# A transformer-trunk layer on one Trainium2 core: another model of the engines orders the instruction queues

## The chip, the cores and the metric

The kernel runs on one core of a Trainium2 chip. The core has five engines with a queue of instructions each, which run their queues strictly in order and wait for one another through semaphores: TensorE (PE in the profile, with PEld for its weight loads), VectorE (DVE), ScalarE (ACT), GpSimd (POOL) and SyncE (SP), which only issues transfers; POOL issues some too. The metric is the device time of one execution in microseconds (us). A queue's order is fixed when the program is built, so a ready instruction waits as long as the one ahead of it on its engine does.

## What is computed

One layer of a decoder trunk over 520 columns: 512 tokens of a prompt and 8 samples of one token each, with 1024 features, in float32. Cut to its core the reference is:

```
sh1, sc1, g1, sh2, sc2, g2 = split(silu(c) @ ada_w + ada_b)
h  = rms_norm(x) * (1 + sc1) + sh1
xr, gr, q, k, v, fl, ga, gb = split(h @ w_in)
hr = rg_lru(causal_dwconv(xr))                  # gates, a scan over time
ya = (hr * gelu(gr)) @ w_proj_a
yb = attention_with_forget_gates(q, k, v, log_sigmoid(fl + b_f)) @ w_proj_b   # samples: paged cache
x  = x + g1 * ((sigmoid(ga) * ya + sigmoid(gb) * yb) @ w_o)
h2 = rms_norm(x) * (1 + sc2) + sh2
gu, up = split(h2 @ w_ffn_in)
y  = rms_norm(x + g2 * ((silu(gu) * up) @ w_ffn_out))
```

## The kernel before

Features lie on the 128 partitions (8 blocks), columns on the free axis, in two halves of 260. Each float32 product is made of three matmuls of a faster type: an operand is split into a high part (a cast) and a low part (the rest), and high x high, low x high and high x low are summed in one PSUM bank (`half_product`, L274 to L281). Weights go through the same steps all along: a transfer into `wraw` (`load_chunks`, L193; two buffers), a cast on ACT into `whi` (L226), a subtraction on DVE into `wlo` (L228; three buffers each), and then the matmuls. PSUM has 8 banks of one tag (`bank`), handed out in turn. Seven buffers of the tag `pg` serve in turn the modulation weights (`araw`), the pages of the cache (`pg`) and sums of weight blocks (`ws`).

The stages in the order of the code:

- Head. x is loaded, normalised (`ss`, `r`, `xn`), and the first two modulation vectors come from eight `araw` transfers of 512 KB for each half of the features (`first_mod`, L449, matmuls L452). `first_mod_end` copies the result (`adas`, L458), transposes it (`adaft`, L461) and makes `mod` (L465) and `n1amp` (L469). `first_h` (L475 to L480) forms `hh` and `hl`, the two parts of h, on ACT, POOL and DVE. The weights of q come through `q_weights` (L486 transfer, L493 cast, L494 subtraction), and its matmuls are at L503. `cs` is a table of constants, of which a second part (128x432) is loaded at L561.
- 50 to 120 us. The other pieces of the modulation (`ada`, transfers L332, matmuls L344), the forget logits (`pfl`, L600), weights of the gates (L865, L866), the log1p chains of the decay (L566 to L574).
- 100 to 360 us. The branch with the recurrence (`xr`, taps `xc` L934, its parts `xch` L314 and `xcl` L315, gate matmuls L955, the scan L979, copies to the output `rg_out` L991) and the merge gates (`ga`), while DVE multiplies the samples' key pages by q and sums them up (L702 to L707).
- 360 to 660 us. Attention, the projections, the merge, `w_o`, the second norm.
- 660 us to the end. The feed-forward layer. Its first tiles are plain: `fi0` to `fi3` and `fig2`, `fiu2`, `fig3`, `fiu3`, of which `swish` (L1469, ACT) reads the `fig` banks and `times_up` (L1473, DVE) the `fiu` banks. The others are made by `fast_tile` (matmuls L1569), seven products of sums of blocks in place of eight. For these POOL forms, once, sums of h2 for k = 0 to 3 (`h2_blocks`: `b1`, `b2` at L1542, `u` and `w` at L1543 to L1546), which ACT and DVE split into `tuh`/`twh` (L314) and `tul`/`twl` (L315), and, for each tile, sums of weight blocks `ws` (`split_block`, L241 to L244), which ACT and DVE split into `wb` (L248, L249).

The two pieces of POOL's work in that last stage are:

```
b1, b2, u, w = (slot(n) for n in ("b1", "b2", "u", "w"))
for b, (hi, lo) in ((b1, h2[k]), (b2, h2[k + 4])):
    pool.tensor_tensor(b, hi.bitcast(F32), lo.bitcast(F32), ALU.add)      # L1542
...
pool.tensor_tensor(s1, a21, a22, ALU.add)                                 # L241, ws
```

What sets the order: the code issues instructions for all engines in program order, with a few orders written out by hand (`issue_after` on page loads and some subtractions); then the framework's scheduler decides, when the context of L1680 closes, in which order each engine's queue holds them, respecting all data and buffer dependencies. It does so with a model of how long each instruction takes.

## Time and profile before

| what | value |
|---|---|
| median of three runs | 1056.56 us (1054.35 to 1057.24) |
| span of the profiled execution | 1055.0 us |
| mean granted TensorE clock in it | 0.982 |
| TensorE busy | 1005.1 us, 95% |
| DVE, ACT, POOL busy | 74%, 50%, 29% |

The time of the profiled execution itself is not among the three; its span runs from its first instruction to its last. Views used below are the page of this execution; the table of busy time by stretches (each row gives the stretch, its length, busy us and the instruction count of each engine, the granted clock, the DMA engines' share and GB/s); and the order of work on each engine (start, duration, engine, line, operation, output and inputs, shapes, count; in square brackets the idle time ahead of it and what ended that). SPq rows are transfers being issued by SP's queue; their duration is the issuing, not the transfer.

### The profile page before, as it was taken

How to read it: one execution, taken by the hardware profiler on the slowest of the kernel's cores; microseconds unless marked ns; L12 is line 12 of the kernel's file. 1: busy time of each engine (PE TensorE's matmuls, PEld its weight loads, DVE VectorE, ACT ScalarE, POOL GpSimd, SP SyncE). 2: the span in 40 equal slices, each digit the busy share in tenths (PEclk: the TensorE clock that was granted, in tenths of full speed). 3: DMA queues.
4: the chain of work that ended last, by engine and by line, in shares of the span. 5: the costliest groups of instructions: out<-in, count | busy, mean ns of one | idle time of the engine just before them, and what ended most of it. 6: DMA issues, size and time to landing. Idle time of an engine off the chain costs nothing.

```text
span 1055.0 us, 21248 instructions
## 1 busy us (share of the span) xinstructions
PE 1005.1 (95%) x8054; PEld 929.9 (88%) x8054; DVE 777.6 (74%) x1370; ACT 530.0 (50%) x1070; POOL 310.3 (29%) x419
## 2 busy tenths in 40 slices
PE   4999999999999999999999999997999999999993
PEld 1788899999898988878888989987999999999993
DVE  4547999988989978867655547748578558869663
ACT  3523665847671467668783235525244324524351
POOL 0324511112133245644400014383134024223114
PEclk8999999999999999999999999998999999999997
DMA  9887987788888999886865852221343233233212
GB/s 320 294 298 283 299 282 221 261 244 266 275 236 310 338 311 291 297 278 209 278 227 189 311 166 71 56 65 61 100 111 91 90 111 104 68 116 102 83 51 82
DMA packets 165354, 206.98 MB, mean 196 GB/s; under 512 B 9842, under 2 KB 126082, under 8 KB 165186
## 3 DMA queue, kind: packets, MB, share of 16 engines
q1 hardware_dynamic: 148530, 152.52, 46.0%
q0 software_dynamic: 13040, 46.67, 13.3%
q10 hardware_dynamic: 3680, 6.42, 1.7%
q8 instruction: 63, 1.03, 0.4%
q14 instruction: 41, 0.34, 0.1%
HBM read 192.49 MB, written 13.09 MB: 195 GB/s over the span
## 4 chain that ended last, share of the span: by engine, by line
PE 73%; DVE 10%; ACT 5%; DMA 4%; issue 3%; POOL 3%; SPq 0%; POOLq 0%; DVEq 0%; ACTq 0%
PE fo L281 11%; PE fi_S L1569 7%; PE fi_A L1569 6%; PE pb L281 4%; PE gb L281 4%; PE pa L281 4%; PE k L281 3%; PE ga L281 3%; PE v L281 3%; PE fiu L281 3%; PE fig L281 3%; PE wo L281 3%; PE gr L281 2%; PE xr L281 2%; PE pv L791 2%
## 5 line engine op out<-in xcount | busy, mean ns | idle before, releaser
L226 ACT CAST whi<-wraw 128x1024 fp32r<-128x1024 f32 (+2 forms) x113 | 111.5, 987 | 188.1 <-PE fo L281 45.1
L228 DVE TENSOR_TENSOR wlo<-wraw,whi 128x1024 fp32r<-128x1024 f32 (+2 forms) x113 | 134.9, 1194 | 50.5 <-ACT whi L226 43.9
L281 PE MATMUL fo<-ach,whi 128*128 128x260 f32 x302 | 85.7, 284 | 0.0
L281 PE MATMUL fo<-ach,wlo 128*128 128x260 f32 x302 | 85.2, 282 | 0.0
L281 PE MATMUL fo<-acl,whi 128*128 128x260 f32 x302 | 85.1, 282 | 0.0
L658 POOL DMA_DIRECT2D pg<-in_cache_k_dram x74 | 39.4, 533 | 142.7 <-DVE S L707 70.3
L241 POOL TENSOR_TENSOR ws<-wraw 128x512 f32<-128x512 f32 x13 | 17.6, 1350 | 200.5 <-DMA wraw<-in_w_fi_dram 197.2
L706 DVE TENSOR_TENSOR pg<-pg,qb 128x1024 f32<-128x1024 f32 x48 | 58.0, 1227 | 1.9 <-DMA pg<-in_cache_k_dram 1.8
L707 DVE TENSOR_REDUCE S<-pg 128x16 f32<-128x1024 f32 x48 | 57.0, 1207 | 0.1
L281 PEld LDWEIGHTS fo<-ach,whi 128*128 128x128 f32 x302 | 56.9, 188 | 0.2
L281 PEld LDWEIGHTS fo<-ach,wlo 128*128 128x128 f32 x302 | 56.9, 188 | 0.0
L281 PEld LDWEIGHTS fo<-acl,whi 128*128 128x128 f32 x302 | 56.8, 188 | 0.0
L1191 POOL TENSOR_SCALAR p<-p,mu 128x128 f32<-128x128 f32 (+3 forms) x28 | 36.4, 1310 | 47.9 <-DVE mu L1187 31.1
L1569 PE MATMUL fi_A<-h2h,wb 128*128 128x260 f32 x208 | 40.2, 294 | 8.7 <-ACT sw L1469 8.7
L249 DVE TENSOR_TENSOR wb<-ws,wb 128x512 fp32r<-128x512 f32 x52 | 44.3, 862 | 3.9 <-ACT wb L248 3.7
L373 POOL TENSOR_TENSOR ss<-ss,sq 128x260 f32<-128x260 f32 x18 | 13.6, 755 | 111.0 <-ACT sq L372 110.6
L248 ACT CAST wb<-ws 128x512 fp32r<-128x512 f32 x52 | 31.4, 620 | 24.0 <-issue 7.3
L1185 ACT ACTIVATE p<-p,mu 128x128 f32<-128x128 f32 (+3 forms) x64 | 35.3, 552 | 15.3 <-DVE mu L1184 15.0
L1569 PEld LDWEIGHTS fi_A<-h2h,wb 128*128 128x128 f32 x208 | 33.8, 199 | 9.0 <-ACT sw L1469 9.0
L248 ACT CAST wb<-wraw 128x512 fp32r<-128x512 f32 x39 | 23.8, 619 | 33.7 <-PE fo L281 18.1
L1396 DVE SCALAR_TENSOR_TENSOR x<-fo,mod,x 128x252 f32<-128x252 f32 x32 | 15.3, 477 | 32.9 <-PE fo L281 32.9
L1569 PE MATMUL fi_S<-twh,wb 128*128 128x260 f32 x208 | 38.4, 285 | 0.0
(436 smaller groups left out, 4068.5 us busy)
## 6 DMA issues: line engine op xcount, KB each, us to landing
araw<-in_ada_w_dram SPq DMA_DIRECT2D x48, 512.0 KB, 7.2
wraw<-in_w_fi_dram SPq DMA_DIRECT2D x44, 512.0 KB, 5.1
pg<-in_cache_k_dram POOLq DMA_DIRECT2D x42, 512.0 KB, 6.0
pg<-in_cache_v_dram SPq DMA_DIRECT2D x42, 512.0 KB, 4.7
wraw<-in_w_in_dram SPq DMA_DIRECT2D x34, 512.0 KB, 8.2
wraw<-in_w_in_dram SPq DMA_DIRECT2D x11, 1024.0 KB, 9.9
pg<-in_cache_v_dram POOLq DMA_DIRECT2D x22, 512.0 KB, 6.1
pg<-in_cache_k_dram POOLq DMA_DIRECT2D x32, 256.0 KB, 5.6
```

Of the source, the lines that this page charges most:

```text
L226: state["act"] = act.copy(hi[:, :k1 - k0], src)
L228: state["last"] = dve.tensor_tensor(lo[:, :k1 - k0], src, hi[:, :k1 - k0].bitcast(F32), ALU.subtract)
L248: state["act"] = act.copy(t[:, :4], src)
L249: state["last"] = dve.tensor_tensor(t[:, 4:], src, t[:, :4].bitcast(F32), ALU.subtract)
L281: state["mm"] = pe.matmul(out[:, :HALF], lhsT=wt[k], rhs=at, start=k == 0 and m == 0, stop=k == nk - 1 and m == 2)
L658: done.append(eng.dma_start(pg, cache[bass.ds(r, 1), :, c0:c1].rearrange("a p c -> (a p) c")))
L706: dve.tensor_tensor(pg, pg, q, ALU.mult)
L707: last = dve.tensor_reduce(S[r // 2][:, c:c + H], pg.rearrange("p (h d) -> p h d", d=DH), AX.X, ALU.add)
L791: pe.matmul(pv[0][32 * gq:32 * gq + 32, :], lhsT=pw[r][:, c:c + 32], rhs=pgs[gq // 2][:, 512 * hf:512 * hf + 512], start=j == 0, stop=j == ...
L1185: act.activation(p[:, :n + 128], p[:, :n + 128], AF.Exp, bias=mu[:, 0:1], scale=-1.0, accum_out=mu[:, 1:2])
L1191: (pool.tensor_scalar(p, p, mu[:, 2:3], None, ALU.mult) if a and i + 1 < KT else act.activation(p, p, AF.Copy, scale=mu[:, 2:3]))
L1569: state["mm"] = pe.matmul(b, lhsT=wt[k], rhs=at, start=k == 0 and m == 0, stop=k == 3 and m == 2)
```

## The change

```
-    with tile.TileContext(nc) as tc:
+    with tile.TileContext(nc, schedule_with_timeline_sim=True) as tc:
         tile_trunk_kernel(tc, *args)
```

The option makes the scheduler order the queues by a more detailed model of the engines in time. The instructions, their tiles and their transfers are the same; only ACT has two loads of a function table fewer (35 instead of 37), since functions of one table stand together more often. What differs is the place of an instruction on its own engine's queue. In the new program about one in ten of PE's instructions and most of those of DVE, ACT, POOL and SP up to 730 us stand in another place, by a few places mostly; behind that the orders of DVE, ACT and POOL are the same but for details.

The places that the prediction speaks of, in the order of the new queues:

SP, at the head (in the order before, all eight `araw` of the first half came first, then the three `wraw`, then the next `araw`, and `cs` came after these):

```
araw x7   L449
wraw x3   L486
cs        L561
araw      L449   (the eighth of the first half)
b_f, pvm
araw x6   L449   (second half)
wraw x3   L486
araw x2   L449
araw x4   L332   (ada), then x2
flr, araw, gates' weights x2, wraw (L193), gates' weights x6, qd x3, araw, araw, qd, araw
```

PE, before `pfl`: `ada` on six `araw` (L344), then `pfl` (L600) twice; before, one pair of these `ada` stood behind `pfl`, one behind the next q products, and one 13 us later.

POOL, from 672 us (before: all of k = 0 up to the second `w`, then `ws` L241, `u` of k = 0, `ws` L242 to L244, then k = 1 to 3, with the second set's L241 ahead of the last `u` and L242 to L244 behind it):

```
ws L241, ws L243               (first set; need wraw)
b1, b2 of k = 0, ws L242, u, w, ws L244, w, u
ws L241, ws L243               (second set; need the next wraw)
b1, b2 of k = 1, ws L242, u, w, ws L244, w, u
b1, b2, u, w, w, u of k = 2
b1, b2, u, w, w, u of k = 3
```

ACT, in the same stretch (before: `tuh`, `twh` of k = 0, `whi`, those of k = 1 and 2, two `wb` from `wraw`, those of k = 3, then the swish of `fig2`, and the other `wb` among what follows):

```
whi, wb x2 (from wraw), tuh, twh of k = 0, wb x4
tuh, twh of k = 1, 2 and 3
sw (swish of fig2, both halves)
```

In the middle, DVE's page products and sums (L702 to L707), the subtractions for `wlo` and `xcl`, the taps of `xc` and the scans are interleaved in another order; on ACT `rg_out` (L991) stands ahead of some casts that it stood behind; on PE the matmuls of the gates with `xcl` (L955) stand some matmuls later, inside the next `ga` product.

## The prediction

> **What bounds the kernel now.** I read the page first, then a table of busy time by stage, then the order of work on single engines where TensorE (PE) stops.
>
> ```profile
> span 1055.0 us, 21248 instructions
> PE 1005.1 (95%) x8054; PEld 929.9 (88%) x8054; DVE 777.6 (74%) x1370; ACT 530.0 (50%) x1070; POOL 310.3 (29%) x419
> PEclk8999999999999999999999999998999999999997
> ```
>
> The sum below is made against this execution's span of 1055.0 us; the median of the three runs is 1.56 us longer, which I take as what lies around the span and add at the end. PE is the bound on average. Where it is not, the table by stage tells (columns: stretch, its length, busy us and instruction count of PE, weight loads, DVE, ACT, POOL; then granted clock, DMA share, GB/s).
>
> ```profile
> 0.00:60.00 60.00, 44.64 (x342) 32.23 (x343) 31.12 (x49) 26.33 (x51) 10.53 (x26) 0.91 0.86 293
> 60.00:120.00 60.00, 58.20 (x466) 50.05 (x465) 40.55 (x84) 21.88 (x46) 24.11 (x48) 1.00 0.87 299
> 120.00:180.00 60.00, 60.00 (x478) 56.11 (x477) 59.41 (x89) 36.75 (x71) 10.96 (x21) 1.00 0.82 264
> 300.00:360.00 60.00, 58.19 (x476) 54.41 (x475) 59.37 (x76) 21.01 (x34) 21.15 (x35) 1.00 0.96 294
> 660.00:720.00 60.00, 49.66 (x398) 48.60 (x397) 37.51 (x53) 22.34 (x46) 41.10 (x49) 0.95 0.20 54
> 780.00:840.00 60.00, 60.00 (x503) 60.00 (x502) 45.01 (x77) 27.57 (x52) 12.64 (x8) 1.00 0.37 106
> sum 1055.00, PE 1005.12 PEld 929.91 DVE 777.59 ACT 529.98 POOL 310.34; mean PE 55.84 PEld 51.66 DVE 43.20 ACT 29.44 POOL 17.24
> ```
>
> So PE loses 15 us at the head, 1.8 us in 60 to 120, 10.3 us in 660 to 720, and nothing from 780 on, where a 260-column matmul takes 60/503 = 0.119 us. A delay that arises before 720 cannot be made up behind it. From 120 to 360 DVE is as full as PE. Since the edit reorders queues and changes no instruction but two table loads of ACT, I went through the new order on each engine and asked at each of PE's stops, and wherever an instruction was put behind one that starts later in this trace, whether PE has to wait.
>
> **Step A, the head.** The eight `araw` transfers feed the eight steps of `adaf`; PE's wait for each ends with its landing (columns of the order of work: start, us, engine, line, operation, tiles, count, idle time before and what ended it).
>
> ```profile
> 8.11 8.57 SPq L449 DMA_DIRECT2D araw<-in_ada_w_dram  x8
> 16.72 3.65 SPq L486 DMA_DIRECT2D wraw<-in_w_in_dram  x3
> 22.43 1.08 PE L452 MATMUL adaf<-araw,silc 128*32 128x256 f32 x8 [0.27 <-DMA araw<-in_ada_w_dram]
> 23.80 1.08 PE L452 MATMUL adaf<-araw,silc 128*32 128x256 f32 x8 [0.29 <-DMA araw<-in_ada_w_dram]
> 24.95 0.37 ACT L458 COPY adas<-adaf 128x256 f32<-128x256 f32 x1 [9.20 <-PE adaf L452]
> 26.56 0.81 ACT L475 ACTIVATE hh<-xn,mod,n1amp 128x512 fp32r<-128x512 f32 x1
> 27.43 0.58 PE L503 MATMUL qp<-hh,whi 128*128 128x260 f32 x1 [1.36 <-ACT hh L475]
> ```
>
> The steps come 23.80 - 22.43 = 1.37 us apart, which is the pace of one 512-KB transfer. In the new order the eighth `araw` stands on SP behind the three `wraw` (512 KB each) and the second part of `cs` (128x432, 216 KB). At the rate of the stretch in which these land,
>
> ```profile
> 25.00:30.00 5.00, 3.26 (x12) 2.67 (x13) 3.79 (x9) 4.40 (x9) 3.16 (x6) 0.50 1.06 378
> ```
>
> 378 GB/s, the three take 3 x 1.39 us and `cs` 0.59 us, so the eighth lands 4.7 us later. The chain from 23.80 through `adas`, `adaft`, `mod`, `hh` to the first `qp` at 27.43 hangs on it whole and moves with it. Something comes back: the `whi` and `wlo` casts that now stand between the `hh` would be done already. But PE's clock is 0.50 in this stretch, and at half clock (0.238 us a matmul) the dozen `qp` matmuls that follow would hardly run faster with their weights ready, so I take back 0.3 us. Price +4.4 us; bounds 0 (if the transfers do not land in the order of issue) and 4.7. PE is full behind it, so it stays.
>
> **Step B, the pieces of `ada` (L344).**
>
> ```profile
> 74.07 1.06 PE L344 MATMUL ada<-araw,silc 128*32 128x512 f32 x8
> 87.32 1.06 PE L344 MATMUL ada<-araw,silc 128*32 128x512 f32 x8
> ```
>
> These two groups and one between them (six transfers) stand in one block ahead of `pfl` in the new order. The first three transfers move ahead of a `wraw` on SP that waits for DVE; the last three do not. Bounds 0 and 13 us (87.32 - 74.07, the last piece landing no earlier than it is used now). I take +0.5, near the lower, because A shifts PE's need by 4 us and the transfers ahead of the last are gone earlier.
>
> **Step C, 100 to 660 us.** The order moves DVE's page products, casts and tap sums past each other, ACT's copies of `rg_out` (L991) ahead of casts, and the `xcl` halves of the gate matmuls (L955) back behind some `ga` matmuls, which loosens waits such as this one:
>
> ```profile
> 282.28 0.51 PE L955 MATMUL gate<-xch,gws 128*128 128x260 f32 x2 [1.83 <-ACT gate L956]
> ```
>
> It is the same work on an engine that is 59.4 of 60 us busy, so some waits go and others come. Bounds: all of PE's losses from 60 to 660 vanish (about 8 us), or several new waits of 2 to 4 us (+15). I take +1.0, a little above nothing: at some ten places a cast is put behind an instruction that was ready later than PE needed the cast, mostly by 1 to 3 us, and A's 4 us cover most of these.
>
> **Step D, 660 to 730 us, the largest term.** PE stops because its next matmul needs a PSUM bank, and the eight are held by `fig2` to `fiu3` until ACT's swish (L1469) reads the first.
>
> ```profile
> 709.24 0.28 PE L281 MATMUL fiu<-h2l,whi 128*128 128x260 f32 x1
> 718.26 0.80 PE L1569 MATMUL fi_A<-h2h,wb 128*128 128x260 f32 x2 [8.75 <-ACT sw L1469]
> 723.63 0.64 PE L1569 MATMUL fi_S<-twh,wb 128*128 128x260 f32 x2
> 716.77 0.62 ACT L314 CAST tuh<-u 128x520 fp32r<-128x520 f32 x1 [6.11 <-POOL u L1546]
> 717.83 0.66 ACT L1469 ACTIVATE sw<-fig 128x260 f32<-128x260 f32 x2
> 672.96 2.62 POOL L1542 TENSOR_TENSOR b<-h2h,h2l 128x520 f32<-128x520 f32 x2
> 677.31 0.92 POOL L1545 TENSOR_TENSOR w<-b,u 128x260 f32<-128x260 f32 x1
> 688.94 1.28 POOL L241 TENSOR_TENSOR ws<-wraw 128x512 f32<-128x512 f32 x1 [10.71 <-DMA wraw<-in_w_fi_dram]
> 699.09 0.73 POOL L1543 TENSOR_TENSOR u<-b 128x260 f32<-128x260 f32 x1
> 711.38 1.18 POOL L1543 TENSOR_TENSOR u<-b 128x260 f32<-128x260 f32 x1
> 716.01 0.73 POOL L1546 TENSOR_TENSOR u<-b,w 128x260 f32<-128x260 f32 x1
> 716.70 1.27 POOL L242 TENSOR_TENSOR ws<-ws,wraw 128x512 f32<-128x512 f32 x1
> 719.63 1.74 POOL L244 TENSOR_TENSOR ws<-wraw,ws 128x512 f32<-128x512 f32 x1
> 662.83 34.87 SPq L193 DMA_DIRECT2D wraw<-in_w_fi_dram  x6
> 681.84 1.23 DVE L228 TENSOR_TENSOR wlo<-wraw,whi 128x1024 fp32r<-128x1024 f32 x1 [0.65 <-ACT whi L226]
> 711.89 2.35 DVE L249 TENSOR_TENSOR wb<-wraw,wb 128x512 fp32r<-128x512 f32 x2
> ```
>
> The swish is ready at 709, but stands on ACT behind the casts of `u` and `w` of block 3, which wait for POOL's last `u` (ends 716.74). POOL works without a pause from the landing of `wraw` at 688.94 to there, 27.80 us. In the new order two `ws` operations on that `wraw` (L241, L243) stand ahead of all of `h2_blocks`, so the first five operations of block 0 (672.96 to 678.23, 5.27 us) no longer fill POOL's wait of 10.71 us; and L242 to L244 of the second `ws` set (716.70 to 721.37, 4.67 us), now behind the last `u`, come ahead of it. On ACT the swish keeps its place behind those casts. The last `u` ends at 688.94 + 27.80 + 5.27 + 4.67 = 726.68: +9.9 us. The second set's `wraw` is the last of the six issues that end at 697.70, and POOL reaches it some 12 us behind 688.94, about when it lands. Behind the stall the clock restarts cold as now: the 24 matmuls from 718.26 to 723.63 take 5.4 us instead of 2.9, no new cost.
>
> Bounds by POOL's own rows: 8 `b` at 1.31, 16 short operations at 0.73 and the two sets at 5.95 give 34.1 us and +6.3; the short ones at 1.18 give 41.3 and +13.5. I take +9.9, since the same mix of DVE work runs beside it. [...]
>
> Sum: 4.4 + 0.5 + 1.0 + 9.9 = +15.8 us, a span of 1070.8 and a time of 1072.4 us (+1.5%).
>
> **The rivals.**
>
> 1. Not slower, through the landing at 688.94. If that `wraw` landed by 673, POOL's 37.74 us would end at 710.7, 6.0 us earlier than now, and pay for A to C: 1056.6; with some of the 8 us of PE's lost time from 60 to 660 gone too, down to 1049. It decides from a landing before 679 on, where D's price falls under zero. For it: POOL does stand idle there. Against it: the transfer waits for the `wlo` that ends at 683.07 and frees one of two buffers, and that part of the order is unchanged.
> 2. DVE and ACT become the bound in the middle. With DVE at 59.41 and 59.37 of 60 us, a matmul moved ahead of its cast waits in full, and a stop as long as the one in D adds 2.5 us of cold clock. Four or five of them, 10 to 15 us more: 1084. For it: `rg_out` copies wait for DVE's scan with casts behind them. Against: `xcl` is loosened, and PE's own delay from A gives the others 4 us of slack.
> 3. Only part of D is paid, because POOL's operations run at their short prices, and PE regains 4 us in the middle: 15.8 - 3.6 - 4 = +8, about 1065 and down to 1060.
> 4. The order on the queues makes no difference that counts, as each engine waits for the same data: 1056.6.
>
> **How the numbers follow.** Forecast (1065 to 1079) 0.58; rival 1 0.10; rival 2 0.20; rival 3 0.09; rival 4 0.03. A difference under 0.3% (3.2 us) cannot be told from none. Slower: 0.58 + 0.20 + 0.09 = 0.87; same: 0.03 of rival 4 and 0.02 of rival 1; faster: 0.08 of rival 1. The range 1060 to 1087 leaves out rivals 1 and 4 and the upper quarter of rival 2, 0.18 in all.
>
> **What would show it.** A: the first `qp` matmul at 32 instead of 27.4, with the eighth `adaf` step waiting for its DMA behind a wait of about 5 us. B: a wait of under 2 us ahead of `pfl`. C: PE's losses from 100 to 660 within a few us of now. D: POOL idle until the landing, its last `u` 37 to 38 us behind it, and PE's stop before the first `fi_A` at 18 to 20 us instead of 9. The stretches behind 735 should be equal but shifted. It is wrong if the stop in D does not grow, or if PE from 100 to 360 loses over 8 us more than now.

## The result, and the profile after

The changed kernel takes 1075.49 us (median of 4 runs, 1072.84 to 1077.8); the kernel before, run beside it on the same chip, 1056.08 (4 runs). The ratio is 1.0176, 95% interval 1.0153 to 1.0199: slower by 1.8%, where 1072.4 us and slower were forecast.

The page of the changed kernel, the lines that answer to those shown of before:

```profile
span 1074.2 us, 21222 instructions
...
PE 1006.2 (94%) x8054; PEld 931.7 (87%) x8054; DVE 773.6 (72%) x1370; ACT 529.3 (49%) x1068; POOL 311.7 (29%) x419
...
PEclk9899999999899999999999999996999999999997
```

Every engine has nearly the same work as before. PE has 1.1 us more of it and the span 19.2 us more, so the time is in PE's stops. Where they lie, the table of busy time by stretches of the changed kernel tells (columns as in the prediction):

```profile
0.00:60.00 60.00, 38.80 (x297) 26.66 (x297) 28.40 (x44) 24.19 (x44) 5.76 (x23) 0.89 0.89 309
60.00:120.00 60.00, 59.35 (x475) 51.50 (x474) 40.50 (x84) 21.82 (x50) 26.65 (x50) 1.00 0.87 288
...
240.00:300.00 60.00, 55.09 (x430) 50.50 (x429) 54.63 (x68) 35.64 (x64) 11.61 (x22) 0.94 0.91 289
...
480.00:540.00 60.00, 57.51 (x432) 49.18 (x432) 36.37 (x86) 42.01 (x104) 27.81 (x46) 0.97 0.73 228
...
660.00:720.00 60.00, 59.08 (x491) 58.84 (x490) 41.70 (x77) 26.37 (x55) 33.90 (x43) 1.00 0.27 71
720.00:780.00 60.00, 41.07 (x328) 40.86 (x327) 36.58 (x68) 21.18 (x41) 18.20 (x18) 0.83 0.20 62
780.00:840.00 60.00, 60.00 (x503) 60.00 (x502) 49.06 (x84) 25.67 (x50) 24.57 (x16) 1.00 0.36 98
```

The stretch 660 to 720 looks cured only because everything comes some 12 us later: its loss of 10.3 us has become one of 18.9 in 720 to 780. Stretches of fixed limits mislead once the work has moved. What can be compared is the same matmul in both traces. For each stage, the start of its first matmul on PE, from the span's start (the last row is the end of the last matmul):

| first matmul of | before, us | after, us | later by |
|---|---|---|---|
| `qp` (head) | 27.4 | 31.6 | 4.2 |
| `xr` | 96.4 | 103.3 | 6.9 |
| `ga` of tile 5 | 225.6 | 232.1 | 6.5 |
| `ga` of tile 7 | 283.5 | 293.6 | 10.1 |
| `k` of tile 6 | 488.9 | 499.6 | 10.7 |
| `k` of tile 7 | 512.1 | 525.1 | 13.0 |
| `fig2` | 686.3 | 697.8 | 11.5 |
| first `fi_A` | 718.3 | 740.0 | 21.7 |
| `fo2` | 925.4 | 946.3 | 20.8 |
| end | 1040.4 | 1059.6 | 19.2 |

By the steps of the prediction: A and B (to `xr`) 6.9 us against 4.9 forecast, C (`xr` to `fig2`) 4.6 against 1.0, D (`fig2` to `fi_A`) 10.2 against 9.9, behind it -2.5 against 0; together 19.2 against 15.8. The rows of D, POOL's first and last in its run, ACT's and PE's at its end:

```profile
700.50 1.29 POOL L241 TENSOR_TENSOR ws<-wraw 128x512 f32<-128x512 f32 x1 [15.06 <-DMA wraw<-in_w_fi_dram]
...
737.71 0.73 POOL L1546 TENSOR_TENSOR u<-b,w 128x260 f32<-128x260 f32 x1
...
738.47 0.62 ACT L314 CAST tuh<-u 128x520 fp32r<-128x520 f32 x1 [5.12 <-POOL u L1546]
739.53 0.66 ACT L1469 ACTIVATE sw<-fig 128x260 f32<-128x260 f32 x2
739.96 0.80 PE L1569 MATMUL fi_A<-h2h,wb 128*128 128x260 f32 x2 [18.93 <-ACT sw L1469]
```

POOL waits 15.06 us for the landing, works from 700.50 to 738.44 = 37.94 us (27.80 + 5.27 + 4.67 = 37.74 was the sum), ACT casts the last `u` and `w`, then comes the swish, then PE: the chain as forecast, stop included (18 to 20 us).

The rows of A:

```profile
12.63 4.27 SPq L486 DMA_DIRECT2D wraw<-in_w_in_dram  x3
16.95 2.76 SPq L561 DMA_DIRECT2D cs<-in_cst_dram  x1
19.82 0.49 SPq L449 DMA_DIRECT2D araw<-in_ada_w_dram  x1
28.02 1.08 PE L452 MATMUL adaf<-araw,silc 128*32 128x256 f32 x8 [5.82 <-DMA araw<-in_ada_w_dram]
...
31.64 0.59 PE L503 MATMUL qp<-hh,whi 128*128 128x260 f32 x1 [1.36 <-ACT hh L475]
```

The eighth `adaf` step waits 5.82 us for its transfer, and the first `qp` starts at 31.64 (32 was forecast).

### The profile page after: what moved, and what is told of

The parts are those of the page before. It is cut to its first block, busy times and chain, and to the rows that moved or that the text cites. A ratio compares the mean times of both kernels' runs of the same rounds, so it can differ in the third digit from the quotient of the medians.

```text
span 1074.2 us, 21222 instructions
## 1 busy us (share of the span) xinstructions
PE 1006.2 (94%) x8054; PEld 931.7 (87%) x8054; DVE 773.6 (72%) x1370; ACT 529.3 (49%) x1068; POOL 311.7 (29%) x419
## 3 DMA queue, kind: packets, MB, share of 16 engines
q0 software_dynamic: 13040, 46.67, 13.1%
## 4 chain that ended last, share of the span: by engine, by line
PE 75%; DVE 7%; ACT 5%; POOL 4%; DMA 4%; issue 3%; SPq 1%; POOLq 0%; DVEq 0%; ACTq 0%
PE fo L281 10%; PE fi_S L1569 7%; PE fi_A L1569 5%; PE wo L281 4%; PE pb L281 4%; PE gb L281 4%; PE ga L281 4%; PE k L281 4%; PE v L281 3%; PE xr L281 3%; PE fiu L281 3%; PE fig L281 3%; PE gr L281 2%; PE pv L791 2%; PE qp L503 2%
## 5 line engine op out<-in xcount | busy, mean ns | idle before, releaser
L228 DVE TENSOR_TENSOR wlo<-wraw,whi 128x1024 fp32r<-128x1024 f32 (+2 forms) x113 | 131.5, 1163 | 72.9 <-ACT whi L226 64.5
L241 POOL TENSOR_TENSOR ws<-wraw 128x512 f32<-128x512 f32 x13 | 17.0, 1305 | 207.8 <-DMA wraw<-in_w_fi_dram 189.6
L1569 PE MATMUL fi_A<-h2h,wb 128*128 128x260 f32 x208 | 39.8, 292 | 18.9 <-ACT sw L1469 18.9
L707 DVE TENSOR_REDUCE S<-pg 128x16 f32<-128x1024 f32 x48 | 57.1, 1205 | 0.0
L249 DVE TENSOR_TENSOR wb<-ws,wb 128x512 fp32r<-128x512 f32 x52 | 44.7, 871 | 4.3 <-ACT wb L248 4.2
L1185 ACT ACTIVATE p<-p,mu 128x128 f32<-128x128 f32 (+3 forms) x64 | 35.4, 554 | 16.3 <-DVE mu L1184 15.8
L1191 POOL TENSOR_SCALAR p<-p,mu 128x128 f32<-128x128 f32 (+3 forms) x28 | 32.9, 1187 | 35.6 <-DVE mu L1187 20.6
L281 PE MATMUL k<-hh,whi 128*128 128x260 f32 x128 | 38.1, 298 | 2.2 <-DVE ol L1238 2.2
L249 DVE TENSOR_TENSOR wb<-wraw,wb 128x512 fp32r<-128x512 f32 x39 | 34.4, 884 | 7.2 <-ACT wb L248 7.0
```

The source lines that it names most:

```text
L228: state["last"] = dve.tensor_tensor(lo[:, :k1 - k0], src, hi[:, :k1 - k0].bitcast(F32), ALU.subtract)
L249: state["last"] = dve.tensor_tensor(t[:, 4:], src, t[:, :4].bitcast(F32), ALU.subtract)
L281: state["mm"] = pe.matmul(out[:, :HALF], lhsT=wt[k], rhs=at, start=k == 0 and m == 0, stop=k == nk - 1 and m == 2)
L707: last = dve.tensor_reduce(S[r // 2][:, c:c + H], pg.rearrange("p (h d) -> p h d", d=DH), AX.X, ALU.add)
L1185: act.activation(p[:, :n + 128], p[:, :n + 128], AF.Exp, bias=mu[:, 0:1], scale=-1.0, accum_out=mu[:, 1:2])
L1191: (pool.tensor_scalar(p, p, mu[:, 2:3], None, ALU.mult) if a and i + 1 < KT else act.activation(p, p, AF.Copy, scale=mu[:, 2:3]))
```

## The experiments

Ratios are to the kernel before, run in turn with each on the same chip. `issue_after` is a hint of the order for the scheduler, which then keeps one instruction behind another on its engine; the arithmetic is never touched. Where one stage is compared, it is by the shift of its first matmul against before's trace, as in the table above:

| kernel | ratio (95% interval) | span | `qp` | `xr` | `ga` 7 | `fig2` | `fi_A` | end |
|---|---|---|---|---|---|---|---|---|
| after | 1.0176 (1.0153 to 1.0199) | 1074.2 | 4.2 | 6.9 | 10.1 | 11.5 | 21.7 | 19.2 |
| 1: after, D undone | 1.0136 (1.0105 to 1.0166) | 1070.1 | 4.5 | 8.0 | 11.1 | 13.6 | 16.6 | 15.0 |
| 2: after, head undone | 1.0149 (1.0117 to 1.0181) | 1071.2 | 0.9 | 3.2 | 6.4 | 8.2 | 18.4 | 16.2 |
| 3: after, both undone | 1.0116 (1.009 to 1.0142) | 1068.1 | 0.5 | 2.8 | 6.1 | 12.8 | 15.8 | 13.1 |
| 4: before, blocks first | 0.9936 (0.9916 to 0.9956) | 1050.3 | -1.4 | 0.0 | 1.4 | 4.2 | -4.7 | -4.7 |
| 5: after, taps first | 1.0113 (1.0087 to 1.0139) | 1065.8 | 3.9 | 4.9 | 4.0 | 3.8 | 14.1 | 10.8 |
| 6: after, `fb` first | 1.013 (1.0099 to 1.016) | 1074.3 | 3.4 | 5.3 | 8.5 | 12.5 | 21.6 | 19.0 |
| 7: before, head changed | 1.0047 (1.0024 to 1.0069) | 1063.4 | 2.5 | 3.2 | 6.5 | 9.1 | 9.3 | 8.4 |
| 8: before, swish and sets moved | 0.9951 (0.9928 to 0.9974) | 1050.9 | -0.6 | 0.7 | 1.6 | 1.5 | -7.4 | -4.1 |
| 9: before, swish moved | 1.0011 (0.9998 to 1.0024) | 1057.0 | -2.2 | -1.9 | -1.6 | 0.8 | -8.1 | 2.0 |
| 10: after, four undone | 0.9955 (0.9943 to 0.9967) | 1052.4 | 0.5 | 2.8 | 3.9 | 4.9 | -0.9 | -2.9 |

### 1. D undone

The four `ws` operations of each set go back to the place on POOL that they had before, or nearly: the first set behind `w` of k = 0, the second behind `w` of k = 3.

```
+    blocks, blocks_w, sets = {}, [], []
+        blocks_w.append(pool.tensor_tensor(w[:, L_], b2[:, R_], u[:, L_], ALU.subtract))   # L1545
-            pool.tensor_tensor(s1, a21, a22, ALU.add)
+            with tc.issue_after(blocks_w[0 if not sets else 3].ins): pool.tensor_tensor(s1, a21, a22, ALU.add)
...                                                # and so for s2, s3, s4
```

> The changed order, but POOL forms the weight sums (L241 to L244) where the kernel before has them: the first set behind the second w of block 0, the second set behind that of block 3. Nothing else moves but two or four casts beside them. Theory (the delays of the stages add on PE's path): the last u comes 27 to 29 us behind the landing of wraw instead of 37.9, PE's stop ahead of the first fi_A goes from 18.9 back to about 9 us, and the time falls by 10 us, from 1075.5 to 1065.5 (1064 to 1067). Rival (another wait stands behind this one, casts of wb or a late second transfer): the stop stays above 13 us and the time above 1069.

Measured: the last stage gives back 7.2 of its 10.2 us (`fig2` to `fi_A` +3.0, and the same in run 3), but the time falls by only 0.40%, some 4 us where 10 were expected. In its trace `fig2` starts 2.1 us later than in the changed kernel's, ahead of the place of the edit and with the same queues up to there, and 0.9 us less comes back behind `fi_A`; 7.2 - 2.1 - 0.9 = 4.2. POOL's run in the changed kernel with D undone:

```profile
702.67 1.29 POOL L241 TENSOR_TENSOR ws<-wraw 128x512 f32<-128x512 f32 x1 [11.37 <-DMA wraw<-in_w_fi_dram]
...
731.43 1.26 POOL L243 TENSOR_TENSOR ws<-wraw 128x512 f32<-128x512 f32 x1
732.65 0.73 POOL L1546 TENSOR_TENSOR u<-b,w 128x260 f32<-128x260 f32 x1
```

It takes 30.7 us instead of 27.80: 1.26 us for an L243 that in before stands behind the last `u`, and 1.6 us in longer operations. Beside them DVE (the third of the busy times) works more than in before; these stretches are POOL's run in before and in run 1:

```profile
688.90:716.80 27.90, 20.62 (x172) 20.41 (x170) 13.04 (x9) 5.58 (x10) 27.70 (x25) 0.95 0.14 38
```

```profile
702.60:733.40 30.80, 20.57 (x172) 20.36 (x170) 17.53 (x13) 7.64 (x13) 30.49 (x26) 0.90 0.20 60
```

So the mechanism is shown (the sets' place on POOL moves PE's stop), but the stage is not fully restored. That the longer operations come from the fuller DVE, whose order remains that of the change, fits these rows but was not tried by a run of its own.

### 2 and 3. The head undone, alone and with D

```
+            qw["raw"] = sp.dma_start(raw, ada_w[...])                                       # L449
+        with tc.issue_after(qw["raw"].ins): sp.dma_start(raw[:, ko:ko + 4], w_in[...])      # L486
+    with tc.issue_after(qw["raw"].ins): sp.dma_start(cs[:, C_TRI:], cst[:, C_TRI:])         # L561
```

> The changed order, but the three wraw transfers of the head and cs are issued behind the eighth araw. Theory: the first qp matmul starts at 27.5 instead of 31.6 us, PE's shift of about 5 us at 60 us is gone, and as PE is full behind it the time falls by 4.5 to 5 us, to 1070.5 to 1071. Rival (the middle is bound by DVE and pays back what the head gains): the shift is back by 300 us and the time above 1073.

> Both edits together. Theory: they add up, 15 us less than the changed kernel, 1060.5 (1059 to 1062); what is left against before, about 4 us, is the middle. Rival (each hides a part of the other): 1064 or more.

Measured: the first `qp` starts 0.9 and 0.5 us later than before instead of 4.2, and at `xr` the shift is 3.2 and 2.8 instead of 6.9. The head's order thus costs 3.7 to 4.1 us, and nothing behind it takes that back as far as `ga` 7 (6.4 and 6.1 instead of 10.1). In the time run 2 gains 0.27%, some 3 us where 4.5 to 5 were expected, and the intervals overlap; it is the stages that show it. The two edits together were expected to reach 1060.5 us and reach 1069.86: 13.1 us are still left in the profiled run, of which 10.0 come between `xr` and `fig2`, where 1.0 was forecast. Run 2 has the same queues up to there and takes 5.0, so C is more than the small term of the forecast, but its size varies from run to run. (With the head undone the scheduler also moved some places on PE, ACT, DVE and POOL, mostly up to 480 us.)

### 5 and 6. Two places in the middle

Between `ga` of tile 5 and of tile 7 the changed kernel loses 3.6 us more than before. PE, ACT and DVE around it, in the changed kernel:

```profile
289.27 0.51 PE L955 MATMUL gate<-xch,gws 128*128 128x260 f32 x2 [2.57 <-ACT xch L314]
292.12 1.24 PE L955 MATMUL gate<-xch,gws 128*128 128x260 f32 x4 [2.34 <-ACT gate L956]
288.59 0.62 ACT L314 CAST xch<-xc 128x520 fp32r<-128x520 f32 x1 [1.80 <-DVE xc L934]
...
284.34 1.22 DVE L706 TENSOR_TENSOR pg<-pg,qb 128x1024 f32<-128x1024 f32 x1
...
285.99 0.74 DVE L934 SCALAR_TENSOR_TENSOR xc<-xr,prm,xc 128x510 f32<-128x510 f32 x1
286.65 1.21 DVE L707 TENSOR_REDUCE S<-pg 128x16 f32<-128x1024 f32 x1
287.78 0.74 DVE L934 SCALAR_TENSOR_TENSOR xc<-xr,prm,xc 128x511 f32<-128x511 f32 x1
```

Read from PE back: the gate matmul waits for `xch`, that for the last tap `xc` on DVE, and the taps stand between page products and sums, which nobody needs yet. Run 5 keeps the products behind the taps of tile 7 (`state["last"]` is the instruction behind which the next page product is issued):

```
-            dve.scalar_tensor_tensor(xc[:, d:NP], xr[:, :NP - d], cw[n], xc[:, d:NP], ALU.mult, ALU.add)   # L934
+            t = dve.scalar_tensor_tensor(xc[:, d:NP], xr[:, :NP - d], cw[n], xc[:, d:NP], ALU.mult, ALU.add); state["last"] = t if i == 7 else state["last"]
```

> The changed order, but from the conv of tile 7 on DVE does the taps of xc (L934) ahead of the next page products (L706, L707) instead of behind them. Theory: the two stops of PE at 286 to 292 us (3.17 and 2.62 us between matmuls) come from xch of tile 7, which waits for the last tap; they fall to about 2.4 us in all as in the kernel before, PE's shift between gate7 and ga7 shrinks by 3 to 4 us, and the time by as much, to 1072. Rival (the table load and the sigmoids of L956 set them, whatever DVE does): the stops stay over 5 us in all and the time over 1074.

Measured: the stop at this gate is all but gone; `ga` 7 is 4.0 us late instead of 10.1. Of these 6.1 us, 2.0 were there already at `xr`, so 4.1 are this edit's. The scheduler, given it, also put the `xcl` matmuls of the gates back close to the others on PE and moved some places on the other engines, mostly up to 415 us; the matmuls that waited were those with `xch`. `fig2` too is 3.8 late instead of 11.5, and the intervals of the time are apart (1.0113 against 1.0176). The same row, with the taps first:

```profile
283.80 0.40 PE L955 MATMUL gate<-xch,gws 128*128 128x260 f32 x2
286.23 0.51 PE L955 MATMUL gate<-xch,gws 128*128 128x260 f32 x2 [0.72 <-ACT gate L956]
```

The second place lies ahead of `k` of tile 7 (2.24 us of waiting). There the chain runs back from DVE's `ol`, queued behind a `wlo`, to that one's `whi` on ACT, which stands behind the softmax of a tile (L1185), from there to DVE (L1184) and to POOL, which waits for a transfer:

```profile
508.66 1.27 SPq L658 DMA_DIRECT2D pg<-in_cache_v_dram  x2
509.98 0.42 SPq L1156 DMA_DIRECT2D fb<-ftd  x1
518.26 0.40 POOL L1158 COPY fm<-fb 128x256 f32<-128x256 f32 x1 [4.16 <-DMA fb<-ftd]
519.11 0.29 DVE L1184 CUSTOM_DVE_ANT_0 p<-f,sc 128x128 f32<-128x128 f32 x1 [3.58 <-POOL f L1160]
...
522.14 1.04 ACT L226 CAST whi<-wraw 128x1024 fp32r<-128x1024 f32 x1
525.09 0.39 PE L281 MATMUL k<-hh,whi 128*128 128x260 f32 x1 [2.24 <-DVE ol L1238]
```

The small `fb` stands on SP behind two page loads. Run 6 issues it first:

```
+            state["fb"] = (sp.dma_start(fb, ftd[hd:hd + 1, :].partition_broadcast(128)), i)   # L1156
+        fb = state.get("fb") if eng is sp else None                                           # page loads, L656
+                tc.issue_after(fb[0].ins) if fb and fb[1] == 7 else nullcontext():
```

> The changed order, but the pages that SP loads behind the last two fb (L1156) in program order are issued behind them, not ahead. Theory: the stop of 2.64 us at 522.5 ahead of k7 is the landing of fb passed on through POOL (L1160), DVE (L1184) and ACT's softmax to the cast whi behind it; it goes, and the time falls by 2 to 3 us, to 1073. Rival (the pages are then late and pv waits for them, or the cast waits for something else): no gain, 1075 or more.

Measured: from `k` of tile 6 to that of tile 7 the shift grows by 0.4 us (14.0 to 14.4) instead of 2.3, so the chain was read rightly. The median, 1072.26 us, is near the 1073 expected, but the profiled run, the longest of its four, is no shorter than the changed kernel's, since PE waited elsewhere in it:

```profile
PE pv L793 <- DMA pg<-in_cache_v_dram: 3.0, 2, 2.5
```

(3.0 us in 2 waits, the longest 2.5; the changed kernel has 0.6 in 2.) That wait lies at 359 us, 150 us ahead of the place that the edit is about, and the queues are those of the changed kernel up to 505 us: it is a page that landed later in this run (run 3 has such a wait of 2.71 us at 357 us), not the edit's price. Whether the 2 us gained at `k` show in the time, this run can't tell: the intervals of the ratio with and without the edit overlap.

### 7. The head's change made to the kernel before

```
-    first_mod(0, acc[0], range(KT))
+    first_mod(0, acc[0], range(KT - 1))
-    first_mod_end(0, acc[0])                # and first_h, moved behind the weights of q:
+    first_mod(0, acc[0], (KT - 1,))
+    first_mod_end(0, acc[0])
```

> The kernel before with one thing done: in the head the three wraw transfers of q, and their casts, stand ahead of the eighth araw, as in the changed order (cs stays behind). Theory: the eighth adaf step starts 4.2 us later (three transfers of 1.39 us), the first qp matmul at 31 to 32 us, and the time rises by 3.5 to 5 us, to 1060. Rival (PE's later waits for DVE swallow it): under 2 us, 1058 or less.

Measured: 0.47% or 5.0 us by the ratio, 3.2 us at `xr`, and 8.4 at the end of the profiled run, the longest of its five. The head's part agrees with run 2's 3.7. The rest has two sources that this run does not part: the edit also moved some queue places up to 150 us, and the middle varies from run to run (last section); the largest piece, 4.7 us between `ga` 5 and `ga` 7, is a stretch where the queues are those of before, and in it a `whi` cast on ACT waits 8.92 us for its `wraw` to land.

### 4, 8 and 9. What holds the last stage

In run 4 both sets of `ws` stand behind `w` of k = 3, in the kernel before:

```
+            with tc.issue_after(blocks_w[3].ins): pool.tensor_tensor(s1, a21, a22, ALU.add)
...                                                # and so for s2, s3, s4
```

> The kernel before with only one thing moved: on POOL both sets of weight sums stand behind the last u of the blocks of h2. Theory (PE's stop of 9 us is POOL's wait of 10.7 us passed on by the queue): the last u ends at about 699 instead of 716.7, the stop goes, the clock stays up (2.5 us more), and the time falls by 10 to 11.5 us, to 1045 (1044 to 1047). Rival (the sums of weights are then late, and the product with S2 waits for them): the stop only moves behind the first two products, and the time is 1050 or more.

Measured: `fig2` to `fi_A` falls by 8.9 us, PE's stop ahead of `fi_A` (9.02 us from matmul to matmul in before) is gone but for three waits of under 0.8 us behind it, and the kernel is faster than before by 0.64%: it beats both. The gain is 6.8 us where 10 to 11.5 were expected. POOL no longer waits for the landing with all of k = 1 to 3 queued behind it. Price of it: the short operations, now beside DVE's subtractions, take up to 1.74 us, against 0.73 to 1.20 in before.

```profile
686.74 1.74 POOL L1543 TENSOR_TENSOR u<-b 128x260 f32<-128x260 f32 x1
...
708.53 0.75 POOL L1546 TENSOR_TENSOR u<-b,w 128x260 f32<-128x260 f32 x1
...
718.58 1.62 POOL L244 TENSOR_TENSOR ws<-wraw,ws 128x512 f32<-128x512 f32 x1
```

Is the PSUM bank (the swish behind the casts) the limit, or POOL's run itself? Run 8 issues the blocks of k = 2 and 3 one tile later, so that the swish of `fig2` does not stand behind their casts, and puts the first set behind `w` of k = 1, the second behind `w` of k = 3. Run 9 makes the first of these edits alone:

```
-            if jt == PLAIN:
-                for k in range(4):
+            if jt in (PLAIN, PLAIN + 1):
+                for k in range(2 * (jt - PLAIN), 2 * (jt - PLAIN) + 2):
                     h2_blocks(k)
```

> The kernel before with the blocks of h2 for k = 0 and 1 ahead of the first set of weight sums on POOL, those for k = 2 and 3 behind it, and these two formed in program order behind the swish of fig2, so that ACT's swish does not stand behind their casts. Theory (PE's stop is a bank held by a swish that waits for POOL through ACT's queue): the first fi_A follows the last fiu at once, at 710, the clock stays up, and a wait of at most 2 us remains ahead of S2; 10 to 12 us less than before, 1045. It should beat the kernel in which only the blocks stand first (1050). Rival (POOL's total work of 38 us sets the end of the stage in any order): 1050 or more.

> The kernel before with one edit: the blocks of k = 2 and 3 are issued one tile later, so that the swish of fig2 stands on ACT ahead of their casts; POOL's order stays as before. Theory 1, the PSUM bank held by the swish alone sets the stop: the first fi_A follows the last fiu directly, and the whole stop (9.02 us from matmul to matmul) is gained, 1047 to 1048. Theory 2, POOL's run sets the stage and the swish is only where it shows: the stop moves to the first product that needs the second set's wb; L242 to L244 of that set end 4.67 us behind the last u here, against 717.6 in the run where the set stood ahead, so the stage gains less than the 5.2 us of that run, 1 to 3 us, and the time is 1053 to 1055.5.

Measured: in both the first `fi_A` follows the last `fiu` directly, and both stop some matmuls later, run 8 first and then run 9:

```profile
714.76 0.39 PE L1569 MATMUL fi_S<-twh,wb 128*128 128x260 f32 x1 [0.90 <-ACT wb L248]
...
718.21 0.58 PE L1569 MATMUL fi_S<-twh,wb 128*128 128x260 f32 x1 [3.06 <-DVE wb L249]
```

```profile
723.16 0.59 PE L1569 MATMUL fi_S<-twh,wb 128*128 128x260 f32 x1 [9.85 <-ACT wb L248]
```

In run 9 the stop at `fi_A` is gone whole (`fi_A` 8.9 us earlier from `fig2`), it comes back as 9.85 us at `fi_S`, and the time is that of before. The two rows on ACT ahead of that `fi_S`:

```profile
721.44 0.62 ACT L314 CAST tuh<-u 128x520 fp32r<-128x520 f32 x1 [10.56 <-POOL u L1546]
...
722.50 1.13 ACT L248 CAST wb<-ws 128x512 fp32r<-128x512 f32 x2
```

The `wb` that `fi_S` waits for is of the first set, which POOL had finished at 696.28; its cast stands on ACT behind those of k = 3, as the swish did, and these wait for POOL's last `u`. The product needs `tw` of k = 3 itself from its tenth matmul on. So the swish is where the stop showed, and POOL's last blocks are what released it, in before and here.

What the bank alone is worth, run 9 does not show. The scheduler moved POOL's order in it too (L241 to L243 of the second set ahead of the blocks of k = 3), so "POOL's order stays" in the expectation did not hold, and the last `u` ends at 721.41 instead of 716.74. These 4.67 us are about what PE might have gained with POOL's order kept, which is an estimate. Run 8, which frees the swish as well, was expected to beat run 4 and does not (0.9951 against 0.9936).

### 10. Four places together

The edits of runs 2, 5 and 6 and run 4's order of POOL, on the changed kernel.

> The kernel after with four edits together: the eighth araw ahead of the wraw and cs at the head, the taps of tile 7 ahead of the page products, the last fb ahead of the page loads, and both ws sets behind w of k = 3 on POOL. If the four named places carry the change's loss, each edit gives what it gave alone: head 3.7, taps 6, fb 2.5, and in 660 to 730 the 14.9 us between +10.2 and -4.7, 27 us in all: 1048 to 1052, faster than before. If the middle's loss is spread over many small waits and moves to other places when one is taken away, the head and the last stage alone give 15 to 19 us: 1056 to 1061.

Measured: 1051.0 us (1049.76 to 1054.14), 0.45% faster than before, 23 us under the changed kernel. The time is the first theory's. By stages of the profiled run it is not quite as that theory has it: against the changed kernel the stretch to `xr` gives 4.1 us, the middle 2.4 (8.5 were expected), `fig2` to `fi_A` 16.1 (14.9 expected). In the middle the two places give what they gave alone, 4.1 us at `ga` 7 and 2.3 at `k` of tile 7, but 2.1 are lost between `xr` and `ga` 5 and 1.7 behind `k` of tile 7. This profiled execution was the longest of its six, 3 us above their median.

## Why the prediction was right, and where its terms were off

**A, right.** The eighth `araw` behind four transfers moves the first `qp` by 4.2 us (4.4 forecast); undoing it alone gives back 3.4 there and 3.7 by `xr`. It repeats: the first `qp` starts at 25.2 to 27.4 us in the four traces with the old head (before, 4, 8, 9) and at 30.8 to 31.9 in the four with the new one (after, 1, 5, 6).

**B, too small, by 2.2 us in this pair.** From the first `qp` to `xr` the shift grows by 2.7 us, where 0.5 was taken. Only 0.65 us of it is the wait ahead of the sixth `ada` piece that B spoke of:

```profile
79.32 1.05 PE L344 MATMUL ada<-araw,silc 128*32 128x512 f32 x4 [0.65 <-DMA araw<-in_ada_w_dram]
```

Of the rest 1.3 us arise ahead of the first q products (`q` 5.5 us late, `qp` 4.2). The cause was not tried by a run. With the head undone the shift still grows by 2.4 us here, so most of it isn't the head's. In the same traces as under A the stretch takes 69.0 to 70.4 us in the old order and 70.0 to 72.4 in the new, so its size is not fixed by one pair.

**C, the step that failed: taken as +1.0 "a little above nothing", it measured +4.6.** The prediction counted places where a cast stands behind something late and let A's 4 us of delay cover most of them. Whether it covered the casts was not tried; the large waits that were found had other links: DVE's taps behind page products that are not urgent (run 5: 4.1 us by `ga` 7), and a small transfer behind page loads on SP, with POOL, DVE and ACT between it and the matmul that waits (run 6: about 2 us). Both are chains in which an urgent instruction stands behind one that is merely ready. These two places repeat from trace to trace, the stretch between them does not (lengths in us; before, 4, 8 and 9 have the old order of the middle):

| stretch | old order | changed order | with the place undone |
|---|---|---|---|
| `ga` 5 to `ga` 7 | 57.9 to 59.4 | 61.5 (after, 1, 2, 3, 6) | 57.4 (5, 10) |
| `ga` 7 to `k` of tile 6 | 205.3 to 208.2 | 205.9 to 212.1 (after, 1, 2, 3, 6) | |
| `k` of tile 6 to `k` of tile 7 | 23.2 | 24.6 to 26.5 (after, 1, 2, 3, 5) | 23.5 (6), 23.2 (10) |
| `k` of tile 7 to `fig2` | 174.3 | 171.3 to 172.9 (after, 1, 2, 3, 5, 6) | |

(Run 7, with the old order there too, has 62.7 in the first row, with the late landing named above.) So the two places cost some 2 to 4 us each, some 2 us come back behind them, and much of the rest of C in any one trace is variation. Rival 2 came nearer in that PE waits for DVE's queue; but what the runs moved was a place in that queue, not how full the engine is, and its size, 10 to 15 us, was too large for this stage.

**D, right in mechanism and size.** 10.2 us against 9.9, a POOL run of 37.94 us against 37.74, by the chain forecast. Runs 1 and 4 move it by moving the sets alone, and the stretch from `fig2` to `fi_A` repeats: 41.0 to 42.2 us in the four traces that keep D (after, 2, 5, 6), 35.0 in the two with it undone (1, 3), 32.0 and 32.2 in the two with the old order (before, 7). The part that run 1 did not give back is 1.3 us of an L243 that did not return to its old place and 1.6 us of longer operations. POOL's 128x260 operation took 1.74 us in a row of run 4 beside DVE and 0.75 in one with DVE idle; in before 1.18 beside DVE's L315 and L249, and 0.73 with DVE idle. The +9.9 took DVE's share of POOL's run to stay as it was, and it nearly did (18.66 of 38.00 us busy, 13.04 of 27.90 in before).

**Rival 1** (POOL's longer run paid for by an earlier landing) fell: the landing is 2.7 us behind the start of `fig2`, as before (2.6).

**Behind D** nothing was forecast (the working said that a delay from ahead of 720 us cannot be made up), and 2.5 us came back. That is luck for the sum: B and C together were 5.8 us short, and this took back 2.5 of it; without it the time would have been some 1078 us, near the upper end of the forecast. 0.9 are a shorter cold stretch: the granted clock of the first 5.37 us behind the stop is 0.63 instead of 0.50.

```profile
718.26:723.63 5.37, 5.37 (x25) 5.37 (x25) 5.06 (x9) 2.57 (x7) 3.11 (x2) 0.50 0.01 3
```

```profile
739.96:745.33 5.37, 5.37 (x30) 5.37 (x31) 4.41 (x11) 3.48 (x10) 0.00 (x0) 0.63 0.01 3
```

The first row is of the kernel before, the second of the changed one; 30 matmuls start where 25 did. In run 1, with nearly the changed order, the first 5.40 us behind the stop have 25 matmuls at 0.50 again. What sets the length of the cold stretch is not shown. The other 1.6 us lie in the last 115 us, where all kernels built on the changed one gain 1.5 to 1.8 us; one wait of 0.9 us for `ss` ahead of the last norm is gone there, and the remainder was not followed up.

## What to carry to other kernels

A new order of the queues is judged at the places where the bound engine stops, and the price of each place is a chain to be read back over every queue on it, the transfer queue and the slow side engine included; an instruction that is ready but not urgent holds up whatever urgent one stands behind it (4.1 us by `ga` 7 in run 5). Where an engine's total sets a stage, work that waits for a landing should stand behind work that doesn't: in the old order that alone gained 0.6% (run 4). When the resource at which a stop shows (a PSUM bank) is freed, ask what the next consumer waits for: here it hung on the same producer, and the stop came back a few matmuls later (9.85 us in run 9).

## What the runs showed of the hardware that was not expected

**The middle varies by some us with the order unchanged.** The queues of run 4 are those of before up to 660 us (but for two DVE instructions at 186 us that change places), and yet its profiled run is 4.2 us later at `fig2`, the difference arising between 279 and 404 us. The table of PE's waits in that stretch of run 4 (total us, times, longest) has:

```profile
PE gate L955 <- ACT gate L956: 2.7, 1, 2.7
PE v L281 <- DVE pl L1205: 1.0, 1, 1.0
```

In before's trace the first is 1.8 us and the second isn't there. Ahead of the first place ACT's cast waits in run 4 for its weights to land; the same cast in before waits for PE alone:

```profile
273.53 1.06 ACT L226 CAST whi<-wraw 128x1024 fp32r<-128x1024 f32 x1 [6.54 <-DMA wraw<-in_w_in_dram]
```

```profile
271.92 1.05 ACT L226 CAST whi<-wraw 128x1024 fp32r<-128x1024 f32 x1 [4.86 <-PE gr L281]
```

(The first row is of run 4, the second of before.) That such landings account for the whole 4.2 us is not shown. Runs 2 and 3, with equal queues up to `fig2`, differ by 5.0 us between `xr` and `fig2`. The 14 runs of the kernel before that stand beside runs 5 to 8 spread from 1052.92 to 1060.0 us. A term of a few us in that stage can therefore not be told by one trace; the place of a wait can.

**Some of POOL's and DVE's operations took longer side by side.** In run 4, POOL's 128x260 operation took 1.74 us where DVE ran these two, against 0.75 with DVE idle, and DVE's 128x1024 subtraction, the first of the two, took 1.85 us beside POOL, against 1.23 in the rows of before where POOL is idle (679 to 686 us):

```profile
686.01 1.85 DVE L228 TENSOR_TENSOR wlo<-wraw,whi 128x1024 fp32r<-128x1024 f32 x1
687.78 1.25 DVE L1432 TENSOR_TENSOR acl<-sw,ach 128x520 fp32r<-128x520 f32 x1
```

So POOL's work moved under DVE's was not hidden for free: in run 4 the blocks of k = 1 to 3 took 26 us (683.19 to 709.28, one L241 among them), and the durations of their 12 short operations add up to 14.1 us, those of before to 10.6.
